# When the decay tables of the first batch's retention heads are computed

## The chip, the cores and the metric

The program runs on one core of one Trainium2 chip. The metric is device time in microseconds of one execution. The kernel before takes 1115.53 us, the median of 3 runs (1115.27 to 1115.87).

## The reference

One layer of a bidirectional encoder for two sequences of 512 tokens (called batch 0 and batch 1 in the kernel), width 1024. Normalised and modulated activations `h` go through one input projection; its columns feed windowed attention (8 query heads of 64, 2 key heads) and retention (4 heads of 128). Both results are joined, projected by `w_out`, and followed by a squared-ReLU MLP of width 4096. The part that the change touches is the decay of the retention scores:

```python
def retention_direction(q, k, v, log_g, strict):
    ...
    diff = pos[:, None] - pos[None, :]
    mask = (diff > 0) if strict else (diff >= 0)
    dmat = jnp.where(mask[None], jnp.exp(jnp.maximum(diff, 0.0)[None] * log_g[:, None, None]), 0.0)
    scores = jnp.einsum('bnihd,bnjhd->bnhij', qc, kc) * dmat
    inner = jnp.einsum('bnhij,bnjhe->bnihe', scores, vc)
...
    lg_f = jax.nn.log_sigmoid(decay_fwd.astype(jnp.float32))
    lg_b = jax.nn.log_sigmoid(decay_bwd.astype(jnp.float32))
    y_f = retention_direction(qf, kf, vf, lg_f, False)
    y_b = jnp.flip(retention_direction(jnp.flip(qf, 1), jnp.flip(kf, 1), jnp.flip(vf, 1), lg_b, True), 1)
    y = y_f + y_b
```

A head's decay depends on its number and on the distance of two tokens alone. The kernel computes all 512 by 512 scores of a head at once, and both directions in one, so that it needs one table for each head: 128 rows of 896 distances, of which each block of 128 keys takes a window of 512.

## The kernel before, in words

Every fp32 matrix product is made of three TensorE matmuls over a high and a low part of each operand (`mm3`, L124 to L126: high by high, low by high, high by low). So each operand is split: ScalarE (ACT) casts the high part, VectorE (DVE) subtracts it to get the low part. For a weight `w` these are `wh_w` (L93) and `wl_w` (L101), for a result of a projection L288 and L289, for the retention scores L409 and L410.

The program has these stretches. Up to some 52 us the first projection of batch 0 runs chunk by chunk by a hand-written list (tiles `first_...`), with the splits of keys and queries of the attention behind it (`ks`, L299 to L302; `qs`, L328 and L329). Then projections of batch 0 run as units (`run_units`), and beside them, as *stages*, the attention blocks and the retention heads. After each half of a unit, `between` turns a clock on by one tick, and `tick_stage` moves one of at most two active stages ahead; a stage that yields 1 rests for one tick, which is half a unit. `x_1` of batch 1 is normalised (`xt_1_...`, L275) and modulated into `h_0_1_...` (L278, L281, L284) beside the last units of batch 0, from some 140 to 190 us. From some 195 us batch 1 goes through the same units; from 377 us the output projection of batch 0 runs beside the last retention of batch 1, then that of batch 1, and the MLP from 475 us on.

A retention head (`ret_head`, L395) asks for its table first, then makes scores of four key blocks (`prs`, DVE multiplies them with the table into `rsf`, L407), sums values (`py`), transposes, and normalises (`bn`, `mv`, `rva`, then POOL's power L440, `rnb`, `ryn`). For batch 0 `decay_table` (L511) computes the table: ACT scales the distances by one direction's log decay (L520), DVE takes the smaller of that and the other direction's (L521), ACT exponentiates (L522), and SP's queue stores the result (L523). For batch 1 the stored table is loaded (L516). A table is `dtab_b_h` for batch b and head h; two buffers are there. Nothing in a table depends on the batch's data, only on the distances `dl` and the log decays `lg` and `nlb`, which are there at 48.9 us.

The order on each engine isn't the order of the code. A scheduler takes instructions, with data dependencies and its own estimate of durations, as early as an engine would be free for them; `tc.issue_after(x)` tells it that an instruction is to stand behind the instruction x. `last_of(engine)` (L174) gives the instruction that was written last for an engine. All other moves follow from the scheduler.

Other names below: `raw_x` is a weight as loaded by SP's queue (L88), `raw_adat` a piece of the modulation weights, which DVE reduces with one custom operation (`jka_b`, L170); `kept_...` are split weights stored for batch 1 (L110); `pj_...` is the PSUM tile of a projection, with `rq`, `rk`, `rv` and `rg` for the retention's queries, keys, values and gate; `st`, `pt`, `po` belong to an attention block.

Of the kernel before, what the change touches and what calls it, by code (L numbers as in the profile page):

```python
# [12 lines left out]
AF = mybir.ActivationFunctionType  # L13
# [19 lines left out]
def trunk_kernel(ctx, tc, x0, x1, x0_t, x1_t, params, gate2_bias, w_ada_first, w_ada_t, w_ada_gate2, w_in_first, w_in,  # L33
                 w_in_v, w_out, w_mlp1, w_mlp2, final_g, y0, y1):
    nc = tc.nc
# [17 lines left out]
    def aux_bank(name):  # L53
        return psum.tile([P, 512], F32, tag="aux", name=name, bufs=5)

    def r4(name, dtype=F32R):
        return work.tile([P, 2, 512], dtype, tag="r4", name=name, bufs=N_R4)
# [4 lines left out]
    def f2(name, dtype=F32):  # L62
        return work.tile([P, 512], dtype, tag="f2", name=name, bufs=6)
# [4 lines left out]
    def small(shape, name, tag="small", bufs=24):  # L68
        return work.tile(shape, F32, tag=tag, name=name, bufs=bufs)

    def f(ap):
        return ap.bitcast(F32)
# [49 lines left out]
    def mm3(ps, lhs, rhs, start, stop):  # L122

        nc.tensor.matmul(ps, lhs[0], rhs[0], start=start, stop=False)  # L124
        nc.tensor.matmul(ps, lhs[0], rhs[1], start=False, stop=False)  # L125
        nc.tensor.matmul(ps, lhs[1], rhs[0], start=False, stop=stop)  # L126
# [47 lines left out]
    def last_of(engine):  # L174
        return next(i for i in reversed(nc.cur_bb.bb.instructions) if i.engine == engine)
# [219 lines left out]
    def ret_head(b, h, q_, k_, v_, sg, mix):  # L395
        nm = f"{b}_{h}"
        dtab = decay_table(b, h)
        py = aux_bank(f"py_{nm}")
        sc = [None] * NT

        def scores(sb):
            ssl = slice(sb * P, (sb + 1) * P)
            psc = aux_bank(f"prs_{nm}_{sb}")
            mm3(psc, (k_[:, 0, ssl], k_[:, 1, ssl]), (q_[:, 0, :], q_[:, 1, :]), True, True)
            sf = f2(f"rsf_{nm}_{sb}")
            o = 384 - sb * P
            nc.vector.scalar_tensor_tensor(sf, psc, RHD ** -0.5, dtab[:, o:o + 512], ALU.mult, ALU.mult)  # L407
            sc[sb] = r4(f"rsc_{nm}_{sb}")
            nc.scalar.copy(sc[sb][:, 0, :], sf)  # L409
            nc.vector.tensor_sub(sc[sb][:, 1, :], sf, f(sc[sb][:, 0, :]))  # L410

        def values(sb):
            hsl = slice(h * P, (h + 1) * P)
            mm3(py, (v_[sb][:, 0, hsl], v_[sb][:, 1, hsl]), (sc[sb][:, 0, :], sc[sb][:, 1, :]), sb == 0, sb == NT - 1)

        scores(0)
        yield 1
        scores(1)
        yield 2
        for sb in range(NT):  # L420
            values(sb)
            if sb + 2 < NT:
                scores(sb + 2)
            if sb < NT - 1:
                yield 1
        yt = f2(f"ryt_{nm}")
        nc.scalar.copy(yt, py)
        yield 1
        pn = aux_bank(f"pyn_{nm}")
        for t in range(NT):  # L430
            nc.tensor.transpose(pn[:, t * P:(t + 1) * P], yt[:, t * P:(t + 1) * P], ident)
        mv = small([P, NT, 2], f"mv_{nm}")
        for t in range(NT):
            st = small([P, 6], f"bn_{nm}_{t}")
            nc.vector.bn_stats(st, pn[:, t * P:(t + 1) * P])
            nc.vector.bn_aggr(mv[:, t, :], st)
        va = small([P, NT], f"rva_{nm}")
        nc.vector.tensor_scalar(va, mv[:, :, 1], EPS, None, ALU.add)
        rs = small([P, NT], f"rrs_{nm}")
        nc.gpsimd.tensor_tensor(rs, va, neghalf[:, :NT], ALU.pow)  # L440
        yn = f2(f"ryn_{nm}")
        nb = small([P, NT], f"rnb_{nm}")
        nc.vector.scalar_tensor_tensor(nb, mv[:, :, 0], -1.0, rs, ALU.mult, ALU.mult)
        for t in range(NT):
            nc.scalar.activation(yn[:, t * P:(t + 1) * P], pn[:, t * P:(t + 1) * P], AF.Identity, bias=nb[:, t:t + 1],
                                 scale=rs[:, t:t + 1])
        yield 2
        pb = aux_bank(f"pyb_{nm}")
        for t in range(NT):
            nc.tensor.transpose(pb[:, t * P:(t + 1) * P], yn[:, t * P:(t + 1) * P], ident)  # L450
        nc.vector.scalar_tensor_tensor(mix[2 + h // 2][:, h % 2, :], pb, 0.5, sg, ALU.mult, ALU.mult)
# [4 lines left out]
    dl = mwork.tile([P, TW], F32, name="dl")  # L456
# [21 lines left out]
    lg = const.tile([P, 2, RH], F32, name="lg")  # L478
# [34 lines left out]
    def decay_table(b, h):  # L513
        if b == 1:
            dt = mwork.tile([P, TW], F32, tag="dtab", name=f"dtab_{b}_{h}", bufs=2)
            nc.sync.dma_start(dt, kept_tables[h])  # L516
            return dt
        dt = mwork.tile([P, TW], F32, tag="dtab", name=f"dtab_{b}_{h}", bufs=2)

        nc.scalar.activation(dt, dl, AF.Copy, scale=lg[:, 0, h:h + 1])  # L520
        nc.vector.scalar_tensor_tensor(dt, dl, nlb[:, h:h + 1], dt, ALU.mult, ALU.min)  # L521
        nc.scalar.activation(dt, dt, AF.Exp)  # L522
        nc.sync.dma_start(kept_tables[h], dt)  # L523
        return dt
# [159 lines left out]
    def ret_units(hT, b, h):  # L684
        r = {}
        nm = f"{b}_{h}"

        def dq(bank):
            r["q"] = split2(bank, f"rq_{nm}")

        def dk(bank):
            r["k"] = split2(bank, f"rk_{nm}")

        def dg(bank):
            sg = take_gate(nm, bank)
            if h % 2 == 0:
                mixes[b].append(r4(f"mix_{b}_{2 + h // 2}", F32))
            stages.append(("retention", lambda: ret_head(b, h, r["q"], r["k"], ret_v[b], sg, mixes[b])))
        return [proj_unit(hT, 768 + h * P, f"rq{nm}", dq),
                proj_unit(hT, 1280 + h * P, f"rk{nm}", dk), proj_unit(hT, 2304 + h * P, f"rg{nm}", dg)]  # L700
# [396 lines left out]
    def step_rvs(kq):  # L1097
# [9 lines left out]
                 lg=lambda i: next(logs))  # L1107
# [426 lines left out]
```

## Time and profile before

| | |
|---|---|
| median of 3 runs | 1115.53 us |
| profiled execution | 1115.45 us, of which the trace's span is 1113.7 us |
| PE (TensorE matmul) busy | 1081.6 us, 97% |
| DVE busy | 878.2 us, 79% |
| ACT busy | 502.6 us, 45% |
| mean granted TensorE clock | 0.996 of full speed |

PE is the engine to watch: 32 us of the span are left when it is not busy. A row's first number is the start in microseconds from the span's start, the second the duration; in brackets stands how long the engine was idle just before, and what ended the wait. An x4 says that four such instructions are taken together in the row.

### The profile page before, as it was taken

The numbers are of one execution on the slowest core, as the hardware profiler recorded it, in microseconds if no ns is written. First come the engines' busy times: TensorE is split into PE (matmuls) and PEld (weight loads), VectorE is DVE, ScalarE is ACT, GpSimd is POOL, SyncE is SP. The second block draws the span as 40 slices with busy tenths as digits, with TensorE's granted clock in tenths as the row PEclk, the third lists the DMA queues.
The fourth block names the chain that finished last, engine by engine and source line by source line (L and its number), as shares of the span: only waits on it lengthen the run. The fifth ranks groups of instructions, "written<-read, shape, count | busy, mean of one in ns | idle before, by whom it ended". The sixth has DMA issues, their size and how long they took to land.

```text
span 1113.7 us, 14016 instructions
## 1 busy us (share of the span) xinstructions
PE 1081.6 (97%) x4997; PEld 886.7 (80%) x4997; DVE 878.2 (79%) x1474; ACT 502.6 (45%) x861; POOL 39.4 (4%) x54
## 2 busy tenths in 40 slices
PE   7999999999999999989999999999999999999996
PEld 4777787788888787888788888888887888888885
DVE  8989888878886787889988788876759754599685
ACT  6566666545552443554333333333443732335341
POOL 1000000000000001000000000000000000002012
PEclk9999999999999999999999999999999999999998
DMA  9989697764555698733654445442883556525504
GB/s 371 344 299 322 247 353 268 234 213 155 181 174 177 240 337 304 273 121 123 208 187 157 159 161 187 161 170 97 285 337 114 179 197 191 208 80 185 189 19 151
DMA packets 86746, 232.73 MB, mean 209 GB/s; under 512 B 8578, under 2 KB 20882, under 8 KB 86676
## 3 DMA queue, kind: packets, MB, share of 16 engines
q1 hardware_dynamic: 86228, 231.51, 59.2%
q8 instruction: 39, 0.64, 0.2%
q10 hardware_dynamic: 288, 0.31, 0.1%
q14 instruction: 31, 0.25, 0.1%
q0 software_dynamic: 160, 0.02, 0.0%
HBM read 160.75 MB, written 71.06 MB: 208 GB/s over the span
## 4 chain that ended last, share of the span: by engine, by line
PE 72%; DVE 17%; ACT 4%; DMA 3%; issue 3%; POOL 1%; POOLq 0%; DVEq 0%; ACTq 0%
PE px_None L904 13%; PE x L1319 13%; PE py_None L904 10%; PE y L1319 10%; PE po L124 2%; DVE jka_b L170 2%; PE po L125 2%; PE po L126 2%; PE po L384 2%; PE ppt L377 2%; PE psc L351 1%; PE pj_rq L124 1%; PE pj_rq L126 1%; PE pj_rq L125 1%; DVE jka_f L170 1%
## 5 line engine op out<-in xcount | busy, mean ns | idle before, releaser
L1259 DVE TENSOR_TENSOR uc_l<-ur,uc_h 128x1024 fp32r<-128x1024 f32 x56 | 68.4, 1221 | 52.9 <-ACT uc_h L1259 35.8
L1319 PE MATMUL x<-wc_l,uc_h 128*128 128x512 f32 x256 | 99.8, 390 | 0.8 <-DVE wc_l L1259 0.8
L1319 PE MATMUL x<-wc_h,uc_l 128*128 128x512 f32 x256 | 99.6, 389 | 0.0
L1319 PE MATMUL x<-wc_h,uc_h 128*128 128x512 f32 x256 | 99.3, 389 | 0.0
L1259 ACT CAST uc_h<-ur 128x1024 fp32r<-128x1024 f32 x56 | 58.9, 1051 | 73.9 <-PE x L1319 30.8
L1319 PE MATMUL y<-wc_h,uc_h 128*128 128x512 f32 x192 | 74.7, 389 | 0.0
L1319 PE MATMUL y<-wc_l,uc_h 128*128 128x512 f32 x192 | 74.7, 389 | 0.0
L1319 PE MATMUL y<-wc_h,uc_l 128*128 128x512 f32 x192 | 74.7, 389 | 0.0
L1259 ACT CAST wc_h<-w 128x1024 fp32r<-128x1024 f32 x48 | 50.4, 1050 | 48.0 <-PE x L1319 24.0
L1259 DVE TENSOR_TENSOR wc_l<-w,wc_h 128x1024 fp32r<-128x1024 f32 x48 | 58.5, 1220 | 13.6 <-ACT wc_h L1259 11.4
L1319 PEld LDWEIGHTS x<-wc_l,uc_h 128*128 128x128 f32 x256 | 48.0, 188 | 11.5 <-DVE wc_l L1259 1.6
L1319 PEld LDWEIGHTS x<-wc_h,uc_h 128*128 128x128 f32 x256 | 48.1, 188 | 10.1
L1319 PEld LDWEIGHTS x<-wc_h,uc_l 128*128 128x128 f32 x256 | 48.0, 188 | 9.8
L124 PE MATMUL po<-wh_wo,ms 128*128 128x512 f32 x128 | 50.9, 397 | 0.9 <-DMA wh_wo<-kept_wo 0.6
L125 PE MATMUL po<-wl_wo,ms 128*128 128x512 f32 x128 | 50.0, 391 | 0.0
L126 PE MATMUL po<-wh_wo,ms 128*128 128x512 f32 x128 | 49.4, 390 | 0.0
L170 DVE CUSTOM_DVE_ANT_0 jka_b<-raw_adat,cb,cols 128x1024 bf16<-128x1024 f32 x38 | 48.2, 1279 | 0.1
L809 ACT CAST wc_s4h<-raw_w 128x1024 fp32r<-128x1024 f32 x16 | 16.8, 1052 | 63.0 <-PE px_None L904 36.4
L361 ACT ACTIVATE st<-st,negm 128x256 f32<-128x256 f32 (+1 forms) x64 | 35.2, 553 | 21.2 <-DVE negm L356 21.2
L1319 PEld LDWEIGHTS y<-wc_h,uc_h 128*128 128x128 f32 x192 | 36.0, 188 | 7.5
L1319 PEld LDWEIGHTS y<-wc_l,uc_h 128*128 128x128 f32 x192 | 36.0, 188 | 7.5
L1319 PEld LDWEIGHTS y<-wc_h,uc_l 128*128 128x128 f32 x192 | 36.0, 188 | 7.4
(375 smaller groups left out, 2977.6 us busy)
## 6 DMA issues: line engine op xcount, KB each, us to landing
ur<-spill SPq DMA_DIRECT2D x56, 512.0 KB, 4.5
raw_adat<-in_w_ada_t_dram SPq DMA_DIRECT2D x36, 512.0 KB, 6.0
raw_w<-in_w_mlp_dram SPq DMA_DIRECT2D x32, 512.0 KB, 3.5
spill<-s SPq DMA_DIRECT2D x64, 256.0 KB, 3.0
w<-in_w_mlp_dram SPq DMA_DIRECT2D x32, 512.0 KB, 4.6
spill<-u SPq DMA_DIRECT2D x48, 256.0 KB, 2.0
raw_ada<-in_w_ada_t_dram SPq DMA_DIRECT2D x12, 512.0 KB, 9.6
x<-in_x_dram SPq DMA_DIRECT2D x12, 512.0 KB, 8.5
```

Of the source, the lines that this page charges most:

```text
L124: nc.tensor.matmul(ps, lhs[0], rhs[0], start=start, stop=False)
L125: nc.tensor.matmul(ps, lhs[0], rhs[1], start=False, stop=False)
L126: nc.tensor.matmul(ps, lhs[1], rhs[0], start=False, stop=stop)
L170: nc.vector.tensor_tensor_reduce(junk(f"jka_{name}_{sec}_{kc}_{b}"), t, cb[:, b, :], 1.0, bcol[:, sec * KC + kc:sec * KC + kc + 1] if bias ...
L351: nc.tensor.matmul(psc[:, :w], qs[hh][:, isl], k_[:, s, j0 * P:j1 * P], start=(s == 0), stop=(s == 1))
L361: nc.scalar.activation(st[hh][:, :w], st[hh][:, :w], AF.Exp, bias=negm[:, hh:hh + 1], scale=0.125, accum_out=den[:, hh:hh + 1])
L377: nc.tensor.transpose(pt[:, hh * P:(hh + 1) * P], st[hh][:, jj * P:(jj + 1) * P], ident)
L384: nc.tensor.matmul(po, va[:, j0 + jj, g].rearrange("p s e -> p (s e)"), pts[jj][:, s, :], start=(jj == 0 and s == 0), stop=(jj == nj - 1 a ...
L809: nc.scalar.copy(hi, src)
L904: self.last = nc.tensor.matmul(bank[:, cs], x[:, k, :], y, start=first and k == 0 and i == 0, stop=last and k == 3 and i == 2, skip_group_ ...
L1259: last_split[:] = [nc.scalar.copy(hi, src), nc.vector.tensor_sub(lo, src, f(hi))]
L1319: nc.tensor.matmul(out, left[n][x][:, i, ts_], right[n][y][:, i, :], start=first and i == 0 and k == 0, stop=end and i == 1 and k == 2, sk ...
```

## The change

`ret_head` of batch 0 rests one tick between its table and its first scores, so the table's instructions are written into the program half a unit ahead of the scores, and the table's first ACT instruction is to stand behind the ACT instruction that was written last before it. How many instructions there are, and what they compute, stays the same. Line numbers from L397 on grow by 2, and from L522 on by 3.

```diff
     def ret_head(b, h, q_, k_, v_, sg, mix):
         nm = f"{b}_{h}"
         dtab = decay_table(b, h)
+        if b == 0:
+            yield 1
         py = aux_bank(f"py_{nm}")
...
         dt = mwork.tile([P, TW], F32, tag="dtab", name=f"dtab_{b}_{h}", bufs=2)

-        nc.scalar.activation(dt, dl, AF.Copy, scale=lg[:, 0, h:h + 1])
+        with tc.issue_after(last_of(mybir.EngineType.Activation)):
+            nc.scalar.activation(dt, dl, AF.Copy, scale=lg[:, 0, h:h + 1])
         nc.vector.scalar_tensor_tensor(dt, dl, nlb[:, h:h + 1], dt, ALU.mult, ALU.min)
```

Three places show what moves. First ACT at some 49 us, behind the cast of the first value weight, before:

```order
L93 CAST wh_rv0_0_551<-raw_rv0_0_416 128x1024
L520 ACTIVATE dtab_0_0_1533<-dl_93,lg_96 128x896
L520 ACTIVATE dtab_0_1_1665<-dl_93,lg_96 128x896
L522 ACTIVATE dtab_0_0_1533<-dtab_0_0_1533 128x896
L299 CAST ks_0_0_560<-first_0_265 64x512
L300 CAST ks_0_0_560<-first_0_265 64x512
L308 COPY vt_a0_573<-first_1_279 128x512
L522 ACTIVATE dtab_0_1_1665<-dtab_0_1_1665 128x896
L299 CAST ks_0_1_565<-first_0_265 64x512
L300 CAST ks_0_1_565<-first_0_265 64x512
```

and of the change:

```order
L93 CAST wh_rv0_0_551<-raw_rv0_0_416 128x1024
L299 CAST ks_0_0_560<-first_0_265 64x512
L300 CAST ks_0_0_560<-first_0_265 64x512
L308 COPY vt_a0_573<-first_1_279 128x512
L299 CAST ks_0_1_565<-first_0_265 64x512
L300 CAST ks_0_1_565<-first_0_265 64x512
```

The two tables of heads 0 and 1 are gone from here (their DVE steps from DVE too). They now stand some 110 rows further down, among the last attention block of batch 0 and the casts of `wh_rk0_2` and `wh_rg0_2`.

Second DVE, where `x_1` is scaled for batch 1, at some 169 us, before:

```order
L275 TENSOR_TENSOR xt_1_0_1697<-xt_1_0_1697,rb_1_1772 128x1024
L275 TENSOR_TENSOR xt_1_1_1699<-xt_1_1_1699,rb_1_1772 128x1024
L275 TENSOR_TENSOR xt_1_2_1701<-xt_1_2_1701,rb_1_1772 128x1024
L284 TENSOR_TENSOR h_0_1_0_1814<-hm_0_1_0_1815,h_0_1_0_1814 128x512
L170 ISA jka_b_2_1_1_1819,gm_91<-raw_adat_13_1613,cb_85,cols_82 128x1024
L170 ISA gm_91 128x1
L521 SCALAR_TENSOR_TENSOR dtab_0_2_2022<-dl_93,nlb_97,dtab_0_2_2022 128x896
L335 SCALAR_TENSOR_TENSOR rg_0_2_1838<-rg_0_2_1838,pj_rg0_2_1800 128x512
L435 BN_STATS bn_0_0_0_1857<-pyn_0_0_1851 128x6
L284 TENSOR_TENSOR h_0_1_1_1842<-hm_0_1_1_1843,h_0_1_1_1842 128x512
L170 ISA jka_b_2_2_0_1849,gm_91<-raw_adat_14_1741,cb_85,cols_82 128x1024
```

and of the change, from the first scaling of `x_1` on:

```order
L284 TENSOR_TENSOR h_0_1_0_1802<-hm_0_1_0_1803,h_0_1_0_1802 128x512
L170 ISA jka_b_2_1_1_1807,gm_91<-raw_adat_13_1603,cb_85,cols_82 128x1024
L170 ISA gm_91 128x1
L335 SCALAR_TENSOR_TENSOR rg_0_2_1824<-rg_0_2_1824,pj_rg0_2_1788 128x512
L284 TENSOR_TENSOR h_0_1_1_1828<-hm_0_1_1_1829,h_0_1_1_1828 128x512
L170 ISA jka_b_2_2_0_1835,gm_91<-raw_adat_14_1719,cb_85,cols_82 128x1024
L170 ISA gm_91 128x1
L275 TENSOR_TENSOR xt_1_1_1684<-xt_1_1_1684,rb_1_1750 128x1024
L437 BN_STATS bn_0_0_0_1876<-pyn_0_0_1870 128x6
L275 TENSOR_TENSOR xt_1_2_1686<-xt_1_2_1686,rb_1_1750 128x1024
```

The scalings `xt_1_1` and `xt_1_2`, which followed `xt_1_0` at once, now stand behind splits and two reductions `jka_b`, and the table of head 2 is no longer among them. `xt_1_0` itself stands five rows ahead of the piece shown.

Third ACT beside it, before:

```order
L278 ACTIVATE h_0_1_2_1903<-xt_1_1_1699,mod_s0_89,mod_a0_87 128x512
L427 COPY ryt_0_0_1824<-py_0_0_1538 128x512
L334 ACTIVATE rg_0_2_1838<-pj_rg0_2_1800 128x512
L93 CAST wh_rk0_3_1882<-raw_rk0_3_1880 128x1024
L281 ACTIVATE hm_0_1_1_1843<-xt_1_0_1697,mod_s0_89,mod_a0_87 128x512
```

and of the change:

```order
L429 COPY ryt_0_0_1840<-py_0_0_1616 128x512
L278 ACTIVATE h_0_1_2_1865<-xt_1_1_1684,mod_s0_89,mod_a0_87 128x512
L93 CAST wh_rk0_3_1844<-raw_rk0_3_1842 128x1024
L281 ACTIVATE hm_0_1_2_1866<-xt_1_1_1684,mod_s0_89,mod_a0_87 128x512
L93 CAST wh_rg0_3_1932<-raw_rg0_3_1930 128x1024
```

The cast of `wh_rk0_3` now stands straight behind `h_0_1_2`, which reads `xt_1_1`; before, it stood three rows behind it, with `xt_1_1` long made.

On SP's queue the loads `raw_adat_2` and `raw_adat_3`, which stood behind the store of `wh_rv0_3`, now go out one row earlier, right behind `raw_rk0_0`, and the stores of tables 0 and 1 move from rows 76 and 79 of the queue to rows 97 and 106, behind the tables themselves.

## Rows read from the trace of the kernel before

**Rows 1.** ACT, 48 to 56 us: start, duration, engine, line, operation, tiles.

```profile
48.96 1.98 ACT L520 ACTIVATE dtab<-dl,lg 128x896 f32<-128x896 f32 x2 [1.68 <-DVE lg L507]
...
54.42 0.96 ACT L522 ACTIVATE dtab<-dtab 128x896 f32<-128x896 f32 x1
55.39 0.58 ACT L299 CAST ks<-first 64x512 fp32r<-64x512 f32 x1
```

**Rows 2.** DVE and PE, 50 to 64 us, in order of time.

```profile
50.72 2.21 DVE L521 SCALAR_TENSOR_TENSOR dtab<-dl,nlb,dtab 128x896 f32<-128x896 f32 x2
...
56.60 0.69 DVE L301 TENSOR_TENSOR ks<-first,ks 64x512 fp32r<-64x512 f32 x1 [1.27 <-ACT ks L300]
...
58.15 0.47 PE L124 MATMUL pj_rv<-wh_rv,h 128*128 128x512 f32 x1 [0.82 <-DVE ks L302]
...
60.78 0.47 PE L124 MATMUL pj_rv<-wh_rv,h 128*128 128x512 f32 x1 [0.77 <-DVE qs L329]
...
63.88 0.50 PE L125 MATMUL pj_rv<-wl_rv,h 128*128 128x512 f32 x1 [0.31 <-DVE wl_rv L101]
```

**Rows 3.** SP's queue, DVE and PE, 80 to 92 us, in order of time.

```profile
80.19 1.20 SPq L88 DMA_DIRECT2D raw_adat<-in_w_ada_t_dram  x2
...
86.36 1.28 DVE L170 CUSTOM_DVE_ANT_0 jka_b<-raw_adat,cb,onep 128x1024 bf16<-128x1024 f32 x1 [0.34 <-DMA raw_adat<-in_w_ada_t_dram]
...
91.19 0.50 PE L124 MATMUL pj_rq<-h,wh_rq 128*128 128x512 f32 x1 [0.81 <-DVE rv L289]
```

**Rows 4.** Stretches: busy us of PE, PEld, DVE, ACT, POOL, granted clock, DMA, GB/s.

```profile
130.00:140.00 10.00, 7.49 (x32) 5.85 (x32) 6.60 (x15) 6.28 (x16) 0.00 (x0) 0.83 0.37 138
150.00:180.00 30.00, 30.00 (x138) 24.62 (x136) 29.11 (x53) 21.19 (x33) 1.02 (x1) 1.00 0.85 332
260.00:370.00 110.00, 109.99 (x538) 91.77 (x537) 84.12 (x223) 50.43 (x121) 1.77 (x2) 1.00 0.54 182
```

**Rows 5.** PE, 135 us, in order of time.

```profile
135.47 0.80 PE L126 MATMUL pj_rg<-h,wl_rg 128*128 128x512 f32 x1 [2.51 <-DVE wl_rg L101]
```

**Rows 6.** DVE, ACT, POOL and PE, 169 to 186 us, in order of time.

```profile
169.36 0.68 DVE L410 TENSOR_TENSOR rsc<-rsf,rsc 128x512 fp32r<-128x512 f32 x1
169.96 3.49 DVE L275 TENSOR_TENSOR xt<-xt,rb 128x1024 f32<-128x1024 f32 x3
...
179.66 1.19 DVE L101 TENSOR_TENSOR wl_rk<-raw_rk,wh_rk 128x1024 fp32r<-128x1024 f32 x1
...
184.16 0.16 DVE L443 SCALAR_TENSOR_TENSOR rnb<-mv,rrs 128x4 f32<-128x4 f32 x1 [0.90 <-POOL rrs L440]
...
171.22 0.82 ACT L278 ACTIVATE h<-xt,mod_s,mod_a 128x512 fp32r<-128x512 f32 x1 [2.72 <-DVE xt L275]
...
175.01 1.04 ACT L93 CAST wh_rk<-raw_rk 128x1024 fp32r<-128x1024 f32 x1
...
182.28 1.85 POOL L440 TENSOR_TENSOR rrs<-rva,neghalf 128x4 f32<-128x4 f32 x1 [20.81 <-DVE rva L438]
...
180.91 0.50 PE L126 MATMUL pj_rk<-h,wl_rk 128*128 128x512 f32 x1 [0.61 <-DVE wl_rk L101]
...
184.93 0.33 PE L450 MATMUL pyb<-ident,ryn 128*128 128x128 f32 x1 [0.80 <-ACT ryn L445]
```

**Rows 7.** Waits of PE, 196 to 262 us: total us, times, longest us.

```profile
PE ppt L377 <- DVE mx L353: 0.7, 1, 0.7
PE pyb L450 <- ACT ryn L445: 0.5, 1, 0.5
```

**Rows 8.** Waits of PE, 370 to 480 us.

```profile
PE py L124 <- ACT rsc L409: 1.0, 1, 1.0
PE po L124 <- DMA wh_wo<-kept_wo: 0.6, 1, 0.6
...
PE po L124 <- DVE go L753: 0.3, 1, 0.3
```

**Rows 9.** SP's queue, 104 us, in order of time.

```profile
103.94 0.69 SPq L523 DMA_DIRECT2D kept_t<-dtab  x1
```

## The prediction

> **What bounds the kernel now.** I read first the page's head and its busy times: of a span of 1113.7 us PE is idle for 32; the gaps read below make 9.7 of it, and the others lie before 50 us and behind 475 us, where the change moves nothing. Then I read the stretches: in 150 to 180 us both PE (30.00 of 30) and DVE (29.11) are full, while in 260 to 370 us PE has 109.99 of 110 and DVE has room (84.12) [rows 4]. So the end is set by PE's own work plus its gaps, and the question is which gaps the new order closes and which it opens. The gaps I read from the trace in order of time: at 58 to 64 us [rows 2], 91 us [rows 3], 135 us [rows 5], 180 to 185 us [rows 6], 200 to 255 us [rows 7], 377 to 433 us [rows 8]. Only these can move; no instruction comes or goes, so PE's own work is a constant as long as its clock is.
>
> **The front, 49 to 64 us.** Two tables leave: on ACT two copies (1.98 us) and two exponentials (0.96 each), on DVE 2.21 us [rows 1, 2]. What they held up is seen on ACT: the second exponential starts at 54.42 and the casts of `ks_0_1` follow at 55.39, at once behind it [rows 1]; DVE then sits 1.27 us until the second of them and starts its subtraction at 56.60; and PE waits 0.82 us for it at 58.15, since the new projection takes the bank that `ks` is read from [rows 2]. Without the exponential the casts come 0.97 us sooner, and with the other one gone, behind which the first `ks` casts stood, I estimate 0.3 more: 1.3. DVE's chain (the splits of `ks`, seven of `qs`, then `wl_rv`) has no idle between 56.60 and the third gap, so it comes 1.3 sooner as a whole. PE's three gaps of 0.82, 0.77 and 0.31 are all ended by this chain; by the time of the third, PE is 1.3 earlier and no more. Between 0.97 (the exponential alone) and 1.90 (all three gaps), I take **-1.3**.
>
> **The loads at 91 us.** The loads of `raw_adat_2` and `raw_adat_3` went out at 80.19, and DVE waited 0.34 us for one of them before its reduction at 86.36; behind that stand the splits for which PE waits 0.81 at 91.19 [rows 3]. In the new order they stand behind a load some 5 us earlier and are no longer late. The 0.34 can be given back, the rest of the gap is DVE's own work: between 0 and 0.81, I take **-0.35**.
>
> **The gap of 2.51 us at 135 us** [rows 5] stands in a chain (attention output, a reduction, `wl_rg0_1`) that has the same order as before on both engines. It stays, and so does what follows: the granted clock is 0.83 in 130 to 140 us [rows 4]. One level is 2.4 GHz, the other 1.2; a mean of 0.83 over 10 us is 3.4 us at the lower one, at which PE loses half: **1.7 us** is the price of such a fall, kept for a rival.
>
> **Where the tables arrive, 142 to 205 us.** DVE is full here, so 2.2 us of table work for heads 0 and 1 isn't free as it was at 50 us; table 2 leaves to later (about 1.1). What decides is where single rows stand. Before, `xt_1_0` to `xt_1_2` take 3.49 us from 169.96, 1.16 each, so `xt_1_1` is ready at 172.3, long before the cast of `wh_rk0_3` at 175.01 [rows 6]. Of the new order: four splits of 0.60 (the pitch from 169.36 to 169.96) that stood ahead of `xt_1_0` now stand behind it, so it ends near 171.1 - 2.4 = 168.7. Then come four such splits, `h_0_1_0`, the reduction (1.28, less 0.07 of overlap), `rg_0_2`, `h_0_1_1` and the second reduction: 7 x 0.60 + 2 x 1.21 = 6.6, or 7.6 with the row or two that the scheduler holds for a PSUM bank; then `xt_1_1`, 1.16. It ends at 176.5 to 177.5. `h_0_1_2` on ACT takes 0.82 and the cast 1.04 [rows 6], so `wh_rk0_3` is ready at 178.3 to 179.4. PE, walked with the durations of rows, wants it at about 177.65: a new gap of 0.7 to 1.7. I take 1.65, the upper end, because DVE is full and nothing that it is late by can be made up before this row. `wl_rk0_3` on DVE takes 1.19 more (0.75 of it a gap, where before it was 0.61). Behind it the normalisation of head 0 goes over POOL: 1.85 us there before, and PE waited 0.80 [rows 6]; now its `rva` stands behind the late splits, and I get 1.15 to 1.9, taken as 1.5, and 0.2 for a cast of the attention behind a table's copy. Sum 4.1 against 0.61 + 0.80 and the 0.5 at 204 [rows 6, 7] of before, 1.9: **+2.2**, between 0 (DVE gains on the walk) and +3.
>
> **Behind it.** 205 to 262 us: the wait of 0.7 for `mx` goes with the shifted stages, new ones of up to 0.5 come: **-0.3**. 260 to 370 us has no gap [rows 4] and gets at most 0.5: **+0.2**. In 370 to 480 us the new order has another value product ahead of the first output projection, so the wait of 1.0 on `rsc` goes, and a weight load stands earlier in SP's queue for the 0.6; the 0.3 stays [rows 8]. I take **-1.4**, between -1.9 and +0.5, since new waits can come there as they did at 180.
>
> The stores of tables 0 and 1 (0.69 us of SP's queue [rows 9]) move behind the tables; the queue isn't what the loads near them wait for. Tables 2 and 3 are computed where DVE has room, so their cost is nothing; if that cover were gone it would be 1.1 us each. Batch 1 loads its tables well behind all stores. The tick of rest costs nothing by itself: PE has the units' matmuls to do, and the heads of batch 0 end while those of batch 1 haven't begun; what it costs is by way of the orders above.
>
> **Sum.** -1.3 - 0.35 + 2.2 - 0.3 + 0.2 - 1.4 = -0.95. The profiled execution is 1115.45 us (1113.7 of span and 1.75 around it), 0.08 under the median. It would be 1114.5, and in terms of the median **1114.6 us**: a gain that the measurement (0.2%, 2.2 us, can be told from no change) hardly shows.
>
> **Rivals.** (1) *Faster: the stall at 178 us doesn't come.* What speaks for it: the walk puts it on a few rows of a full DVE, and 1 us of slack there undoes it; the front's gain of 1.3 is safer. Against: DVE at 29.11 of 30 has no slack. Price: the +2.2 becomes 0, so 1112.4. (2) *Slower: the gaps at 178 to 185 us take the clock down.* One mechanism: `wh_rk0_3` behind `h_0_1_2` behind `xt_1_1`, then `wl_rk0_3` and `ryn` within 7 us, about 3.9 us of idle. It decides where these gaps together stop PE as the 2.51 did at 135 us, behind which the clock fell [rows 4, 5]; price 1.7, giving 1116.3, and with a second fall when the stages behind come late as well 1118. Against it: none of the gaps that I foresee is as long in one piece as 2.51, and matmuls run between them. (3) *The front's gain is swallowed.* DVE bounds 150 to 180 us and its sum of work up to there doesn't shrink, so that PE waits there for whatever it won at 58 us; then the sum is -1.3 poorer: 1115.9. For it speaks the same 29.11; against it, DVE idles before (6.60 busy of 10 at 130 to 140 us [rows 4]) and starts 1.3 earlier too. (4) That the change doesn't do what it says is excluded by the orders: the tables have gone from 49 us.
>
> On (2) the Trainium skill speaks too ("TensorE: Matmul & The Clock Gate", Part 1): it says that the lower level is the default and that only sustained activity keeps the clock up. This trace agrees at 135 us; by that rule alone the gaps at 178 to 185 us would cost a second fall and the result would be rival 2's.
>
> **How the numbers follow.** The forecast 0.48, rival 1 0.27, rival 2 0.14, rival 3 0.11. Faster by over 0.2% means under 1113.3: most of rival 1 and the lower tail of the forecast (0.27 x 0.85 + 0.48 x 0.15), 0.30. Slower means over 1117.8: half of rival 2 and the upper tails of the others, where the bounds of the +2.2 and the -1.4 go wrong together (+3 and +0.5), 0.16. The rest, 0.54, is within. The range goes from rival 1, less 0.2 of its own, to the point where rival 2 has its first fall and the -1.4 doesn't come, 1116.3 + 1.4 = 1117.7: 1112.2 to 1117.7.
>
> **What would show it.** Right: the three gaps at 58 to 64 us are 0.6 in sum; PE waits over 1 us for ACT's `wh_rk` near 178; the wait on `rsc` at 377 us is gone; the gap at 135 us is as before. Wrong: no gap over 0.8 in 140 to 205 us (then rival 1), a second stretch with a granted clock under 0.95 (rival 2), or a PE that reaches 142 us 1.5 us sooner and 160 us no sooner (rival 3).

## The result and the profile after

The change is slower: 1117.55 us, the median of 21 runs (1116.20 to 1118.61), against 1115.21 for before (21 runs in the same sessions); the ratio is 1.0023, 95% interval 1.0018 to 1.0029, some 2.5 us. The forecast was a gain of 0.9. The profiled execution of the change is 1116.90 us with a span of 1115.1.

Two traces can't be compared by their spans here. The first 49 us (loads and set-up, the same in all kernels) end at different times from run to run: the 101st matmul starts at 26.77 us in the profile of before and at 27.49 in that of the change, and a second profile of before (experiment 7) has it at 29.80. So I compare gaps of PE and stretches, not times of the day.

The front, change (ACT and PE, in order of time; these answer to [rows 1 to 3]):

```profile
55.50 0.58 ACT L299 CAST ks<-first 64x512 fp32r<-64x512 f32 x1 [0.83 <-DVE ks L302]
...
58.26 0.47 PE L124 MATMUL pj_rv<-wh_rv,h 128*128 128x512 f32 x1 [0.32 <-DVE ks L302]
...
60.89 0.47 PE L124 MATMUL pj_rv<-wh_rv,h 128*128 128x512 f32 x1 [0.67 <-DVE qs L329]
...
64.01 0.50 PE L125 MATMUL pj_rv<-wl_rv,h 128*128 128x512 f32 x1 [0.33 <-DVE wl_rv L101]
...
90.85 0.50 PE L124 MATMUL pj_rq<-h,wh_rq 128*128 128x512 f32 x1 [0.65 <-DVE rv L289]
```

The gaps of 0.82, 0.77, 0.31 and 0.81 are 0.32, 0.67, 0.33 and 0.65 now: 0.58 us won at 58 to 64 us, 0.16 at 91. The casts of `ks_0_1` no longer stand behind a table, but they wait 0.83 us for the subtraction of `ks_0_0`, which reads the same tile (`first_0`).

The stretch around 178 us, change (DVE, ACT and PE, in order of time; [rows 6] are those of before):

```profile
174.52 1.22 DVE L275 TENSOR_TENSOR xt<-xt,rb 128x1024 f32<-128x1024 f32 x1
...
177.56 1.23 DVE L101 TENSOR_TENSOR wl_rk<-raw_rk,wh_rk 128x1024 fp32r<-128x1024 f32 x1
...
175.78 0.81 ACT L278 ACTIVATE h<-xt,mod_s,mod_a 128x512 fp32r<-128x512 f32 x1 [1.70 <-DVE xt L275]
176.50 1.03 ACT L93 CAST wh_rk<-raw_rk 128x1024 fp32r<-128x1024 f32 x1
...
177.58 0.50 PE L124 MATMUL pj_rk<-h,wh_rk 128*128 128x512 f32 x1 [1.71 <-ACT wh_rk L93]
...
178.84 0.79 PE L126 MATMUL pj_rk<-h,wl_rk 128*128 128x512 f32 x1 [0.53 <-DVE wl_rk L101]
```

This is the stall of the prediction, row for row: `xt_1_1` ends at 175.7 on DVE, `h_0_1_2` waits for it, the cast of `wh_rk0_3` stands behind that, and PE waits 1.71 us (1.65 was forecast) and then 0.53 (0.75 was forecast).

The stretches of the change (columns as in [rows 4]):

```profile
130.00:140.00 10.00, 7.49 (x40) 5.95 (x40) 8.28 (x17) 6.81 (x16) 0.00 (x0) 1.00 0.44 151
175.00:185.00 10.00, 7.76 (x29) 5.61 (x28) 8.34 (x18) 5.89 (x11) 1.01 (x1) 0.83 0.56 226
```

The gap of 2.51 us at 135 us is there as before, but in this execution the clock didn't fall behind it (1.00). It fell behind the gaps at 178 us: 0.83 over 10 us. By the working of the prediction that is worth 1.7 us again.

Waits of PE in the change, 196 to 262 us and 370 to 480 us (total us, times, longest us; before: [rows 7, 8]):

```profile
PE pgt L203 <- DVE gm L170: 1.1, 1, 1.1
```

```profile
PE px L259 <- DVE rv_x L251: 1.1, 2, 0.8
PE po L126 <- DVE ms L732: 0.7, 1, 0.7
PE py L907 <- ACT wc_a L812: 0.5, 1, 0.5
PE po L125 <- issue: 0.4, 1, 0.4
PE px L259 <- DVE x L778: 0.3, 1, 0.3
PE pyb L452 <- ACT ryn L447: 0.3, 1, 0.3
```

All three of the waits of before that the prediction spoke of are gone (`rsc`, `wh_wo`, `go`), and five others came; the wait for `wc_a` is in both kernels. In before it is this one:

```profile
PE py L904 <- ACT wc_a L809: 0.5, 1, 0.5
```

What the new waits have in common is, as I read it, the last retention head of batch 1. Its normalisation stands behind the first matmuls of the second output projection now, and ACT makes the squares of the finished rows (`jk`) only behind it; PE's transposes `px` wait for what follows from these squares. Change (ACT and PE, in order of time):

```profile
436.13 1.50 ACT L447 ACTIVATE ryn<-pyn,rnb,rrs 128x128 f32<-128x128 f32 x4 [6.09 <-DVE rnb L445]
436.64 0.33 PE L452 MATMUL pyb<-ident,ryn 128*128 128x128 f32 x1 [0.33 <-ACT ryn L447]
437.51 0.64 ACT L761 ACTIVATE jk<-x 128x512 bf16<-128x512 f32 x1
...
442.02 0.44 PE L259 MATMUL px<-ident,x 128*128 128x128 f32 x2 [0.81 <-DVE rv_x L251]
```

Before (ACT and PE, in order of time):

```profile
430.24 1.51 ACT L445 ACTIVATE ryn<-pyn,rnb,rrs 128x128 f32<-128x128 f32 x4 [6.54 <-DVE rnb L443]
431.51 0.62 PE L450 MATMUL pyb<-ident,ryn 128*128 128x128 f32 x4
432.58 0.63 ACT L758 ACTIVATE jk<-x 128x512 bf16<-128x512 f32 x1 [0.83 <-DVE x L754]
```

The head's last transposes (`pyb`) come 5.1 us later and the squares 4.9, of which 0.7 is the later start of the whole.

Why the head is late follows from the program, by counting the ticks of `between` at which each head starts and ends. The four heads of batch 0 end at ticks 28, 33, 40 and 45 before, and at 29, 35, 43 and 49 with the rest. Only two stages run at a time, so a tick of rest delays all that are queued behind it, and the delays add up. The last attention block of batch 1 ends at tick 67, not 62 (its first matmul starts at 324.7 us in the trace, 308.0 before), and batch 1's heads end at 73, 80, 87 and 95, not 72, 76, 83 and 92. The last half unit of batch 0's output projection is tick 92. So the last head, which ended with it, now has its last three steps behind it, where no unit stands beside them.

### The profile page after: what moved, and what is told of

It reads as the page before. It is cut to its first block, busy times and chain, and to the rows that moved or that the text cites. A ratio compares the mean times of both kernels' runs of the same rounds, so it can differ in the third digit from the quotient of the medians.

```text
span 1115.1 us, 14005 instructions
## 1 busy us (share of the span) xinstructions
PE 1084.0 (97%) x4997; PEld 888.8 (80%) x4997; DVE 878.7 (79%) x1474; ACT 502.6 (45%) x861; POOL 38.5 (3%) x54
## 4 chain that ended last, share of the span: by engine, by line
PE 78%; DVE 15%; issue 2%; ACT 2%; POOL 1%; DMA 0%; POOLq 0%; DVEq 0%; ACTq 0%
PE px_None L907 13%; PE x L1322 13%; PE py_None L907 10%; PE y L1322 10%; PE po L125 2%; PE po L124 2%; PE po L126 2%; PE po L384 2%; PE ppt L377 2%; PE psc L351 1%; PE pj_rk L126 1%; PE pj_rk L124 1%; PE pj_rk L125 1%; PE pj_rq L124 1%; PE pj_rg L126 1%
```

## The experiments

My theory A: the loss has two sources, the rest (late heads) and the stall at 178 us with a fall of the clock, for which both halves of the change are needed. The rival, theory B: the tables' 2.2 us of DVE work, which now fall into a stretch in which DVE is full.

All medians stand beside the runs of before of the same session. Gaps of PE in us, summed from its rows in each trace by stretch (of executions that were profiled, one each; the stretches of experiment 7 are taken 3 us later, as its start is):

| kernel | 50-100 | 100-140 | 140-260 | 260-475 | clock fell at | median | of before |
|---|---|---|---|---|---|---|---|
| before | 2.79 | 2.51 | 2.67 | 1.94 | 135 | 1115.21 | |
| change | 1.96 | 2.52 | 3.30 | 2.98 | 178 | 1117.55 | 1115.21 |
| 1 hold only | 1.98 | 2.51 | 3.17 | 1.75 | 135 | 1115.21 | 1115.32 |
| 2 rest only | 2.86 | 2.51 | 2.03 | 2.88 | 135 | 1115.77 | 1115.32 |
| 3 rest paid back | 1.95 | 2.51 | 4.51 | 1.33 | 499 | 1115.96 | 1115.32 |
| 4 cast first | 1.97 | 2.52 | 2.81 | 3.21 | 135 | 1116.96 | 1115.32 |
| 5 before, one tick | 2.68 | 1.34 | 2.45 | 1.84 | no | 1112.36 | 1115.13 |
| 6 change, one tick | 1.97 | 1.33 | 4.01 | 3.54 | no | 1116.64 | 1115.13 |
| 7 before again | 2.73 | 2.52 | 2.65 | 2.04 | 135 | - | |
| 8 change again | 1.96 | 2.52 | 4.09 | 2.94 | 135 | - | |
| 9 change, third | 1.94 | 2.52 | 3.26 | 3.10 | 135, 178 | - | |
| 10 change, fourth | 1.99 | 2.51 | 3.27 | 2.75 | 135, 178 | - | |
| 11 hold only, one tick | 1.96 | 1.33 | 3.65 | 1.52 | no | 1113.37 | 1114.89 |

**1. Hold only**: the tables' first ACT instruction held back, no rest.

```diff
         dtab = decay_table(b, h)
-        if b == 0:
-            yield 1
```

> Only the half of the change that holds the tables' first ACT instruction back; no tick of rest. Theory A (the loss is made by the rest, which lets the last retention head of batch 1 end 3 ticks later, and by the stall at 178 us, which needs both halves, with a fall of the clock behind it): the front's gaps shrink as with the change (about 1.0 us gained by 100 us), no gap over 1 us near 178 us, the gaps from 370 to 480 us as before (about 2.4): 0.5 to 2 us faster than before. Theory B (the loss is the 2.2 us of table work that now falls into a stretch where DVE is full): 1 to 2.5 us slower than before, with a gap near 178 us as with the change.

Measured: 1115.21 us, ratio 1.0000 (0.9991 to 1.0009). Both theories fail in size: A wanted a gain of 0.5 us or more, B a loss of 1 or more. The front wins 0.81 us, as with the change; the gaps of 140 to 260 us grow by 0.50; none is at 178 us, where the cast of `wh_rk0_3` now stands ahead of `h_0_1_2`. What is left, 0.5 us by the gaps, is too small for the interval of 1 us either way.

**2. Rest only**: the tables of heads 0 and 1 stay at 49 us.

```diff
-        with tc.issue_after(last_of(mybir.EngineType.Activation)):
-            nc.scalar.activation(dt, dl, AF.Copy, scale=lg[:, 0, h:h + 1])
+        nc.scalar.activation(dt, dl, AF.Copy, scale=lg[:, 0, h:h + 1])
```

> Only the tick of rest; the tables of heads 0 and 1 stay at 49 us. Theory A: the front as before; heads end as late as with the change (tick 95 instead of 92), so the gaps from 370 to 480 us sum to 2.5 to 3.5 as with the change; no long gap at 178 us: 0.5 to 1.5 us slower than before. Theory B: within 0.3 us of before.

Measured: 1115.77 us, ratio 1.0004 (0.9995 to 1.0013). The waits behind 370 us are those of the change, with no table moved. Three of its waits (PE, 50 to 475 us):

```profile
PE px L259 <- DVE rv_x L251: 1.1, 2, 0.8
...
PE po L126 <- DVE ms L731: 0.8, 1, 0.8
PE px L259 <- DVE x L777: 0.3, 1, 0.3
```

So the rest makes this part: 2.88 us of gaps in 260 to 475 us against 1.94. The stretch 140 to 260 us is better by 0.64 without the held tables, so the sum is small: 0.45 us between the medians, under the 0.5 to 1.5 of theory A and over the 0.3 of theory B, and the interval holds both.

**3. Rest paid back**: the change, but a head of batch 0 leaves out the tick between its first and second scores, so that all heads end at the ticks of before.

```diff
         scores(0)
-        yield 1
+        if b == 1:
+            yield 1
         scores(1)
```

> The change with the tick paid back: heads of batch 0 leave out the tick between their first and second scores, so that all heads end at the ticks of before. Theory A: front's gain kept, no stall at 178 us (the cast of wh_rk0_3 stands ahead of h_0_1_2), gaps behind 370 us as before: 0.5 to 2 us faster than before. Theory B: 1 to 2.5 us slower than before, as the table work lies in the full stretch.

Measured: 1115.96 us, ratio 1.0007 (0.9998 to 1.0016). The late waits are gone (1.33 us in 260 to 475 us), which confirms the ticks. But it isn't faster than before, as theory A wanted, nor 1 us slower, as theory B did: 4.51 us of gaps stand in 140 to 260 us. Its longest waits of PE, 50 to 475 us:

```profile
PE pyb L453 <- ACT ryn L448: 3.6, 4, 1.2
PE pj_rg L126 <- DVE wl_rg L101: 2.5, 1, 2.5
PE py L124 <- ACT rsc L411: 1.0, 1, 1.0
PE pyn L434 <- ACT ryt L430: 0.9, 1, 0.9
```

With the tables in the full stretch the normalisation of all four heads comes late (before: 1.3 us for `pyb`, in two waits). Theory B has its part: where the tables are held, 140 to 260 us costs 0.5 to 1.8 us more, except in experiment 4 (0.14).

This profile holds one more thing. The clock didn't fall behind the 2.51 us at 135 us but behind two gaps in the MLP, which all thirteen profiles have alike and which are followed by a fall in this one alone (PE, and the stretch behind):

```profile
490.88 0.39 PE L908 MATMUL px<-hch,wc_s4h 128*128 128x256 f32 x1 [1.22 <-DVE u L923]
...
497.92 0.39 PE L908 MATMUL px<-hcl,wc_a 128*128 128x256 f32 x1 [1.73 <-DVE hcl L814]
...
495.00:505.00 10.00, 8.27 (x47) 7.49 (x46) 9.15 (x17) 7.18 (x14) 0.00 (x0) 0.83 0.04 14
```

**4. Cast first**: the change, with `xt_1_1` to `xt_1_3` and the statistics of head 0 held behind `wl_rk0_3` on DVE.

```diff
+        if name == "rk0_3":
+            rk_low.append(last_of(mybir.EngineType.DVE))
...
-            nc.vector.bn_stats(st, pn[:, t * P:(t + 1) * P])
+            if nm == "0_0":
+                with tc.issue_after(rk_low[0]):
+                    nc.vector.bn_stats(st, pn[:, t * P:(t + 1) * P])
...
-                x_scale(xt[kc // 2], rb)
+                if kc >= 2:
+                    with tc.issue_after(rk_low[0]):
+                        x_scale(xt[kc // 2], rb)
...
```

> The change with xt_1_1 to xt_1_3 and the first head's statistics held behind wl_rk0_3, so that the projection pj_rk0_3 waits for less; all else as with the change. Theory A: the two gaps of 1.71 and 0.53 near 178 us shrink to 1.0 or less in sum and the clock stays at 1.00 behind them; so 1.2 us from the gaps and up to 1.7 from the clock: 1 to 3 us faster than the change, within 1.2 us of before. Rival without the clock: at most 1.2 us faster than the change. Theory B: as slow as the change, since the work on DVE is the same.

Measured: 1116.96 us, ratio to before 1.0020 (1.0011 to 1.0029); 0.6 us less than the change. Waits of PE (50 to 475 us):

```profile
PE pyb L460 <- ACT ryn L455: 1.1, 2, 0.7
...
PE pj_rk L130 <- DVE wl_rk L103: 0.5, 1, 0.5
PE pj_rk L128 <- ACT wh_rk L93: 0.5, 1, 0.5
```

The two gaps are 1.0 together and the clock stays up at 178 us in the profile; in 3 of its 11 runs the mean clock was 0.995 or less, in the change's own in 14 of 21. But the gain, 0.6 us, is under the 1 to 3 that theory A expected, and it fits the rival without the clock (at most 1.2); the intervals of the two kernels overlap, so that it can't be told from no gain. The wait for `ryn` (0.7) isn't new: the change has it too where its clock holds (0.80 in experiment 8). So this experiment doesn't show what the clock costs. Why no more than 0.6 us is left of shorter gaps and rarer falls stays open.

**5 and 6. One tick more in the background list**, in before and in the change. `wl_rg0_1` then stands ahead of a reduction, not behind it, and the gap at 135 us is 1.30.

```diff
             which, is_scale = divmod(sec, 3)
+            if (sec, kc) == (0, 6):
+                yield
             for b in bs:
```

> The kernel before with one more tick of rest in the background list ahead of one reduction, so that wl_rg0_1 no longer stands behind a reduction of 1.28 us on DVE. Clock theory (a fall of TensorE's clock costs 1.7 us, and the gap of 2.51 us at 135 us causes about one in each run): the gap becomes about 1.2, the granted clock behind it stays at 1.00 in most runs: 1.3 us from the gap and 1 to 1.7 from the clock, 2 to 3.5 us faster than before. Rival (the clock plays no part in the medians): 1 to 1.5 us faster.

> The change with the same extra tick of the background list. It also takes one reduction out of the full stretch ahead of wh_rk0_3, whose cast now finds xt_1_1 made. Theory: both long gaps (2.51 at 135 us, 2.24 at 178 us) shrink and the clock stays up at both: 3 to 5 us faster than the change, so 1 to 3 us faster than before and within 1.5 us of the kernel before with the same tick. Rival (the change loses by its late heads alone): 1.3 us faster than the change, still slower than before.

Measured: in before 1112.36 us, ratio 0.9977 (0.9966 to 0.9988), the fastest kernel here, faster than before and the change. Its mean clock is 0.997 or 0.998 in all of 8 runs; of the 2.8 us, 1.2 come from the gap, and the rest is about what a fall costs, as the clock theory expected. The interval, 1.3 to 3.8 us, only just reaches the rival's 1 to 1.5. In the change 1116.64 us, 1.0010 (1.0001 to 1.0019), mean clock 0.997 or 0.998 in all of 11 runs. The theory wanted 3 to 5 us less than the change and a time within 1.5 us of experiment 5; neither came. The rival, late heads alone, is nearer by the time: 0.9 us less than the change (1.3 expected) and still slower than before. By the trace its cause isn't the whole: neither profile shows a fall while PE works, the change still costs 4.3 us (medians), and 2.5 of it are gaps of 50 to 475 us (10.85 against 8.31): +1.56 in 140 to 260 us, +1.70 behind that, -0.71 in the front. The two profiled executions are 3.45 us apart (1115.75 and 1112.30). What makes the rest, 1.8 us of the medians, stays open.

**7 to 10. Before and the change again.**

> The kernel before once more, for a second profile: what in it is chance from run to run. Expected: the start of the projection (the first 49 us) differs by up to 1 us from the first profile, and the gap of 1.13 us at 546 us may be missing; the gaps between 50 and 475 us are the same within 0.2.

> The change once more, for a second profile. Clock theory: two falls of the clock (behind 135 us and behind 178 us) instead of the one of the first profile, and 1.5 us more. Rival: one fall again.

> The change a third time, for a profile of an execution with a mean clock of 0.995 or less, as 14 of its 21 timed runs had. Clock theory: such an execution shows two stretches with a granted clock under 1, behind the gap at 135 us and behind the gaps at 178 us, each worth 1.7 us. Rival: one stretch, longer. An execution at 0.996 or 0.997 tells nothing new.

> As the third, once more, since two of three executions have it: two stretches under 1 by the clock theory, one longer by the rival.

The gaps of before repeat within 0.1 us a stretch; the start of the 101st matmul doesn't (29.80, 3 us later, where up to 1 was expected), and the wait at 546 us is 0.37 (1.13 before). The second profile of the change (1116.72 us) shows one fall, at 135 us, where the clock theory expected two; the third and fourth (1118.31 and 1118.17 us, mean clock 0.995) show two. Stretches of the third:

```profile
130.00:140.00 10.00, 7.50 (x33) 6.17 (x32) 7.48 (x15) 6.88 (x16) 0.00 (x0) 0.83 0.44 147
175.00:185.00 10.00, 7.82 (x28) 5.72 (x27) 8.76 (x19) 4.96 (x8) 1.01 (x1) 0.83 0.76 310
```

and of the second, with the same two gaps at 178 us and the clock up behind them, and the gap that follows (PE):

```profile
130.00:140.00 10.00, 7.49 (x33) 5.88 (x32) 7.35 (x15) 6.65 (x16) 0.00 (x0) 0.83 0.49 156
175.00:185.00 10.00, 6.98 (x33) 4.78 (x31) 8.76 (x19) 4.98 (x10) 1.01 (x1) 1.00 0.63 256
...
184.09 0.33 PE L452 MATMUL pyb<-ident,ryn 128*128 128x128 f32 x1 [0.80 <-ACT ryn L447]
```

So the same gaps are followed by a fall in some executions and not in others; what decides isn't shown. The change offers one place more for it than before, and 490 to 500 us is one in all kernels.

The mean clock of a timed execution tells the falls only roughly. It counts the end of the program too, where the clock is low behind PE's last matmul (0.50 from 1108.1 us on in the profile of before), and this end differs. Of the profiled executions those without another fall have 0.997 or 0.998, those with one 0.995 to 0.997 (0.995 in experiment 3), those with two 0.995. It was 0.995 or less in 6 of 65 runs of before that have it on record, in 16 of 24 of the change (its 21 runs and the three later ones). Of the change, the median is 1118.05 us with such a clock and 1116.72 at 0.996 or 0.997: a second fall goes with some 1.3 us. That it is less than 1.7 is in part since a slower PE waits less: the gap of 0.80 before `pyb` at 184 us in the second profile is missing where the clock has just fallen. At 0.996 or 0.997 before has a median of 1115.34 (52 runs). So at like clocks the change is 1.4 us slower, and the other 0.9 of its 2.3 go with the more frequent low clock.

**11. Hold only, with the extra tick.**

> The held tables without the tick of rest, with the extra tick of the background list. Theory (the 1 us that the held tables win in the front is paid back where DVE is full, 140 to 260 us): within 1 us of the kernel before with the same extra tick (1112.4), so 2 to 4 us faster than before. Rival (the front's gain lasts once the stall at 135 us is gone): 1 us faster than that, 1111.4.

Measured: 1113.37 us, ratio 0.9984 (0.9975 to 0.9993), 1 us above experiment 5 in another session: the front's 0.7 us is paid back by 1.2 in 140 to 260 us (3.65 against 2.45), as the theory said. It is 1.5 us faster than before, not 2 to 4; the rival's 1111.4 lies outside the interval.

## Why the prediction was wrong

The sum was -0.95 and the change costs +2.3 (medians). Three of the four signs of being right came: the wait of over 1 us for `wh_rk`, the end of the wait on `rsc`, the gap at 135 us. The fourth didn't, and the second stretch with a low clock, a sign of being wrong, came in two profiles. By its steps, with the gaps of the third and fourth profiles, which are like most runs:

- **The front, -1.3: right in sign, too large.** -0.58 was measured, and the three gaps sum to 1.32, not 0.6. The step that failed is "I estimate 0.3 more", and that DVE's chain comes sooner as a whole: it was taken that only the tables hold the `ks_0_1` casts. With these gone, they wait for the split of `ks_0_0`.
- **91 us, -0.35.** Measured -0.16.
- **135 us, no change.** The gap is 2.51 us in all of it. That the fall "stays" was too simple: it came in three of four profiles of the change.
- **142 to 205 us, +2.2, and 205 to 262 us, -0.3.** The two gaps at 178 us were walked rightly (2.24 measured, 2.4 forecast); where the clock fell at 135 us, as in the prediction's trace, even the times fit (third profile: PE stops at 177.46 and goes on at 179.11; 177.65 and 178.3 to 179.4 were walked). The third gap, before `pyb`, was 0.8 or nothing, not 1.5, and the 0.2 for the attention didn't come, so that up to 205 us it is +1.1 where the clock holds (experiment 8) and +0.4 where it falls. In 205 to 262 us a wait of 1.07 for `gm` replaced the 0.72 for `mx`: +0.35, not -0.3. Together the gaps of 140 to 260 us grow by 1.4 where the clock holds; by 0.6 where it falls, and 1.7 of slow matmuls with them. The place and the mechanism were right.
- **The clock: the largest failure of a chance.** Rival 2 had the place, the mechanism and the price, and I gave it 0.14. Three of four profiles of the change show the fall at 178 us, two of them as a second one, and 16 of 24 executions have a mean clock of 0.995 or less, against 6 of 65 of before. The argument against it, that no single gap is as long as 2.51, was wrong: 1.65 to 1.71 and 0.53, with two matmuls between, were enough in three of four profiles. The Trainium skill ("TensorE: Matmul & The Clock Gate", Part 1) has the clock follow how busy TensorE was of late; the profiles agree with that in so far as two gaps of 1.71 and 0.53 us stood ahead of the fall, neither as long as 2.51. Why experiment 8 has the same gaps and no fall, no run here shows.
- **370 to 480 us, -1.4: the term that failed.** +1.0 was measured (the gaps of 260 to 475 us are some 2.9 us in the four profiles of the change and 2.0 in the two of before). That is outside even the term's bound of +0.5. The step was "new waits can come there as they did at 180", kept as a bound and not worked out. I read from the order that the old waits go, which they do, and "the tick of rest costs nothing by itself" took the ticks as local. Counted through to the end of the queue of stages, one tick for each of four heads is three ticks for the last head of batch 1, in the one place where nothing covers it. Experiments 2 and 3 show it by the waits, which come with the rest alone and go when the tick is paid back; the medians of these two are too close to before to show it in the time.
- **Rival 3** (the front's gain is swallowed where DVE is full) holds in part: experiments 1 and 11 win 0.7 to 0.8 us at 58 us and give 0.5 to 1.2 back in 140 to 260 us.

Summed with what was measured by the table's stretches: -0.8 in the front and at 91 us, +0.6 in 140 to 260 us, +1.0 behind it, +1.7 for the second fall of the clock: +2.5 for executions with two falls, where those with a mean clock of 0.995 or less are 2.8 above before. That the late heads make the waits behind 370 us is shown. What the second fall costs is read from profiles and mean clocks; no experiment isolates it, since experiment 4 gained too little to tell and experiment 6 moved the gaps as well. That 1117.55 lies within the stated range is no support for the forecast: its upper end, 1117.7, was made of a fall of the clock and of the -1.4 not coming, both held unlikely.

## What to carry to other kernels

A rest or a delay that is put into one of many queued stages is to be counted through to the end of the queue: what it costs is where the last one ends, and whether other work is left there to cover it. Work that moves from a stretch with room on its engine into one in which that engine is full can be paid back there, even if PE's gaps elsewhere shrink: here it was in all kernels with held tables but one. And gaps of 1.7 to 2.5 us in a dense stretch had a second price here, a lower clock behind them in a part of the executions; one profile doesn't show how often, and the mean clocks of many runs show it roughly.

## What the runs showed of the hardware

The same gap of 2.51 us was followed by a granted clock of 0.66 in 135 to 140 us in the third profile of the change and by 1.00 in the first; eight of the ten profiles with this gap have the fall there. Where the gap was 1.30 (experiments 5, 6 and 11), none of three has it. Two gaps of 1.7 and 0.5 us with two matmuls between were followed by a fall in three of four profiles, and the gaps of 1.2 and 1.7 us at 491 and 498 us, some 7 us apart, in one of thirteen. Each fall is 0.83 over 10 us. The mean clock of a run was 0.997 or 0.998 with none of these falls, 0.995 to 0.997 with one and 0.995 with two. The start of the program differs by up to 3 us between executions of the same kernel (101st matmul at 26.77 and 29.80 us in two profiles of before), which alone is more than the effect that was looked for.
